# A block's decay tables loaded behind a clear, and two pairs of PSUM banks exchanged

## The chip, the cores and the metric

The kernel runs on one core of a Trainium2 chip. The metric is the device time of one execution in microseconds; three timed executions of the kernel before took 422.1, 422.23 and 422.89, so the median is 422.23. Its engines are named as in the profile: PE is TensorE (the matrix products), PEld its weight loads, DVE is VectorE, ACT is ScalarE, POOL is GpSimd and SP is SyncE, which here only issues transfers.

## What is computed

One transformer block on 256 tokens of width 1024, all in fp32. In the reference, cut to what matters here:

```
mod = silu(c) @ w_ada + b_ada                  # six rows of 1024: shifts, scales, gates
h = x * (1 + sc1) + sh1
proj = h @ w_in                                # cut into mq mk mv | rq rk rv | rg | g_a g_r
y_a = moba_attention(rotary(mq), rotary(mk), mv)    # 8 heads of 64; one block of 256 keys: causal softmax
y_r = retention(rotate(rq), rotate(rk), rv)         # 4 heads, 128 for queries and keys, 256 for values
y_r = silu(rg) * head_norm(y_r)
y = (sigmoid(g_a) * (y_a @ w_proj_moba) + sigmoid(g_r) * (y_r @ w_proj_ret)) @ w_out
x = layer_norm(alpha * x + g1 * y)
# then a gated feed-forward layer of width 2816 with a short convolution, and a second layer_norm
```

The retention's scores q k^T are multiplied, element by element, by a decay that depends on the distance of the two tokens and on the head, and is zero for later keys. The kernel gets these factors as a table: for each pair of heads 128 partitions with 2 x 384 numbers, 384 KB a pair.

## The kernel before

**Precision and weights.** Every matrix product of the big layers is made of three products of rounded parts: a weight tile comes from HBM as fp32 into a buffer named raw (five of them, 1 MB each), ScalarE copies it rounded into whi, VectorE subtracts and writes the rest into wlo. Activations are split in the same way (AH holds the high and low part of the modulated x; AYa and AYb, A2a and others hold further pairs).

**The start** (L161 to L416). SP issues the weights in a fixed order; the first modulation weights go out by ScalarE's queue. `load_A` fills the five raw buffers and issues x's transposed tiles (AYa<-in_xT, L197) between them. A few products on data that nobody reads (L228, L249) keep TensorE busy till the first weights are there. VectorE computes the modulation of x's first tile with four multiply-and-sum instructions (L274) and a sum (L278), scales x with it (L303), and the products of `x_prod` (L337) begin. They need the high part of the weights (L320), their low part (L323), and the low part of x (L308, L310).

Where the first weights' tile is loaded by ScalarE's queue, the kernel writes one column of it with VectorE first (L210). The load writes the same tile, so it is ordered behind that write.

**The main list.** Behind the start, `main` is a list of 1 MB weight loads and `steps` a list of functions with the products for each half of a load. A loop (L1335) goes through the steps; in each it calls the generators in `sides` three times, prepares the halves that come due some steps later (L1279, L1293), and calls the step's function. All engines get their instructions in the order in which this loop makes them; semaphores hold an instruction back until what it reads has been written and what it overwrites has been read. The first 16 steps are the rotated queries and keys (L134, L138), the next the gates and output projections (L123 to L125).

**The generators.** `mixers` waits for step 7 (SCORES_AT), then issues the decay loads from GpSimd's queue (L1037), and goes on with the attention: scores (L1050), masked maxima (L1059), softmax, transposes, and in the end `attend` (L1072), whose two results lie in PSUM banks 5 and 6 and are split into high and low part by ScalarE (L100) and VectorE (L101). The decays' place in SBUF has no earlier user, and GpSimd has nothing else to do in the meantime.

`retention` follows. Its scores (L1169) of heads 0 and 1 are put into banks 4 and 7, those of heads 2 and 3 into banks 0 and 1. VectorE multiplies them by the decays (L1172), ScalarE and VectorE split them (L1173, L1177), and the value products of head g, nine to a head (`mm3`, so L123 to L125), go into bank VALUES[g], from which ScalarE reads them (L1153). A bank can be written anew when its last reader is through. Behind the value products GpSimd loads x again (L1181).

Of the kernel before, what the change touches and what calls it, by code (L numbers as in the profile page):

```python
# [68 lines left out]
def _body(nc, a, out, pe, act, dve, sp, cst, wts, big, tmp, ps, dram):  # L69
    f = lambda ap: ap.bitcast(F32)  # L70

    def bank(i):
        return ps.tile([128, 512], F32, tag=f"P{i}", name=f"P{i}")
# [6 lines left out]
    def reopen(dt, *names):  # L80
        for n in names:
            pairs[n] = big.tile([128, 2, 2048 if n == "H" else 1024], dt, tag=f"A{n}", name=f"A{n}")

    def slot(n, shape, dt=F32):
        if n in pairs:
            assert pairs[n].dtype == dt
            return pairs[n].rearrange("p e (k t) -> p e k t", k=shape[2])
        if n not in place:
            return big.tile(shape, dt, tag=f"A{n}", name=f"A{n}")
        pair, e = place[n]  # L90
        assert pairs[pair].dtype == dt
        v = pairs[pair][:, e, :math.prod(shape[1:])]
        return v.rearrange("p (a b) -> p a b", a=shape[1]) if len(shape) == 3 else v
# [5 lines left out]
    def split(hi, lo, src):  # L99
        act.activation(hi, src, AF.Copy)  # L100
        dve.tensor_tensor(lo, src, f(hi), OP.subtract)  # L101
# [210 lines left out]
    whl, S = {}, {}  # L312
# [716 lines left out]
    def mixers():  # L1029


        for _ in range(3 * SCORES_AT):
            yield
        v = S["v"]
        S["decay"] = [slot(n, [128, 2, 384]) for n in ("D0", "D1")]
        for i in range(2):
            nc.gpsimd.dma_start(S["decay"][i], a["decay"][i])  # L1037
        st, pt = {}, {}
        blk = [slice(128 * qb, 128 + 256 * qb) for qb in range(2)]

        def scores(h):


            S["sc"] = [bank(b) for b in (4, 7, 5, 6)]
            x = S["rot"][h // 4]
            for qb, c in enumerate(blk):
                for i in range(2):
                    for e in range(4):
                        s = slice(32 * e, 32 * e + 32)
                        pe.matmul(S["sc"][e][:, c], x[s, i, qb * 128:(qb + 1) * 128], x[s, 2 + i, :128 + 128 * qb],  # L1050
                                  start=i == 0, stop=i == 1)

        def maxima(h):

            for e in range(2):
                sm = S["sms"][:, (h + e) % (TL + 2)]
                mx = tmp.tile([128, 8], F32, name="mx", bufs=TL + 2)
                for qb, c in enumerate(blk):
                    dve.tensor_tensor_reduce(out=sm[:, c], in0=S["sc"][h % 4 + e][:, c],  # L1059
                                             in1=consts["mask"][:, 128 - 128 * qb:],  # L1060
                                             scale=-0.125, scalar=3.0e38, op0=OP.add, op1=OP.min,
                                             accum_out=mx[:, 2 + qb:3 + qb])
                st[h + e] = sm, mx

        def attend(h, p):

            for w in range(2):
                pT = [pt.pop(h + 2 * w + e) for e in range(2)]
                for kb, (o, c) in enumerate(((slice(0, 256), slice(0, 256)), (slice(128, 256), slice(256, 384)))):
                    for e in range(2):  # L1070
                        u = h + 2 * w + e
                        pe.matmul(p[64 * e:64 * e + 64, 256 * w + o.start:256 * w + o.stop],  # L1072
                                  v[:, kb, 64 * u:64 * u + 64], pT[e][:, c], start=kb == 0, stop=kb == 1)
            return lambda: split(S["yah"][:, h // 2:h // 2 + 2], S["yal"][:, h // 2:h // 2 + 2],
                                 p.rearrange("p (w t) -> p w t", w=2))

        for i in range(HM + 5):
            yield
            if 0 <= i - 3 < HM:
                sm, mx = st[i - 3]  # L1080
                for qb, c in enumerate(blk):
                    act.activation(sm[:, c], sm[:, c], AF.Copy, scale=mx[:, 6 + qb:7 + qb])
            if i == 7:
                for t in range(2):
                    act.activation(S["rvx"][0][t], S["rv"][t], AF.Copy)
            if 0 <= i - 1 < HM:
                sm, mx = st[i - 1]
                for qb, c in enumerate(blk):
                    act.activation(sm[:, c], sm[:, c], AF.Exp, scale=-1.0, bias=mx[:, 2 + qb:3 + qb],
                                   accum_out=mx[:, 4 + qb:5 + qb])  # L1090
            yield
            if 0 <= i - 1 < HM:
                dve.reciprocal(mx[:, 6:8], mx[:, 4:6])
            if i == HM + 4:
                S["yah"], S["yal"] = [slot(n, [128, 4, 256], F32R) for n in ("5", "15")]
                done = [attend(4 * g, bank(5 + g)) for g in range(2)]
            for h in {6: (0, 1), 9: (2, 3, 4, 5), 11: (6, 7)}.get(i, ()):
                sm, mx = st.pop(h)
                p = bank((4, 7, 4, 7, 5, 6, 4, 7)[h])
                for b in range(3):  # L1100
                    pe.transpose(p[:, b * 128:(b + 1) * 128], sm[:, b * 128:(b + 1) * 128], ident)
                pT = sm if h > 1 else slot(("9a", "9b")[h], [128, 384])
                act.activation(pT, p[:, :384], AF.Copy)
                pt[h] = pT
            if i == 0:
                S["sms"] = slot(11, [128, TL + 2, 384])
            if i in (0, 4):
                scores(i)
            if i == 4:
                reopen(F32R, "Ya", "Yb")  # L1110
                S["rvx"] = [[pairs["Y" + e][:, t] for t in range(2)] for e in "ab"]
            if i in (0, 2, 4, 6):
                maxima(i)
            if i == RET_AT:
                sides.append(retention())
            yield
        for fn in done:
            fn()

    def retention():  # L1120
        rot, decay, sms = S["rot"][2:], S["decay"], S["sms"]
# [2 lines left out]
            yield  # L1124
            yield
        rv, (rvh, rvl) = S["rv"], S["rvx"]
        SCORES, VALUES = ((4, 7), (0, 1)), (5, 6, 4, 7)
        mv = tmp.tile([128, 3, 8], F32, name="mvr", bufs=1)
        square = decay[0][:, 0, :256]
        sd = tmp.tile([128, 8], F32, name="sdr", bufs=1)  # L1130
# [189 lines left out]
    prep_to(FIRST + 2)  # L1320
    evac_B()
    sides = [mixers()]

    def run_sides():
# [148 lines left out]
```

## Time and profile before

| | before |
|---|---|
| median of three runs | 422.23 us |
| the profiled execution's own time | 421.75 us |
| its span | 420.0 us |
| TensorE busy | 412.0 us (98%) |
| VectorE busy | 374.2 us (89%) |
| ScalarE busy | 255.5 us (61%) |
| moved by transfers | 105.73 MB, mean 252 GB/s |
| TensorE's waits for another engine | L228 1.6, L337 1.2, L123 0.8, L885 0.4 us |

The span is that of the program's own instructions; the execution's time is 1.75 us longer. In the rows of the profile stand start and length in us, the engine, the line of the kernel, the operation, and what it writes and reads, with an arrow; x4 is a group of four, whose length is that of the whole group; "[1.61 <-DMA ...]" is the time for which the engine stood before it, and what ended that. The queue q1 is SP's, q10 ScalarE's, q0 GpSimd's. In the list of waits stand the instruction that waited, the one that released it, and the time in total, the number of waits and the longest. The chain that ended last is followed back from the last instruction, at each step to what released it.

### The profile page before, as it was taken

The page shows a single profiled execution, that of the slowest core. Times are in us where ns is not written, and L with a number is a line of the kernel's source. Part 1 is how long each engine was busy: PE and PEld are TensorE (multiplying, and loading weights), DVE is VectorE, ACT ScalarE, POOL GpSimd, SP SyncE. Part 2 cuts the span into 40 slices and gives each one's busy share as a digit, 9 for nine tenths or more (in the row PEclk, how much of TensorE's full clock was granted, in tenths as well). Part 3 has the DMA queues.
Part 4 walks back from the last instruction along what each step waited for, and adds up shares of the span by engine and source line. Part 5 has one row for each costly group of instructions (what it writes and reads, how often), then busy time and mean ns, then how long its engine had stood idle before and what let it go on. Part 6 is the DMA issues. An engine that isn't in the chain of part 4 may idle for free.

```text
span 420.0 us, 5974 instructions
## 1 busy us (share of the span) xinstructions
PE 412.0 (98%) x2168; PEld 346.7 (83%) x2168; DVE 374.2 (89%) x599; ACT 255.5 (61%) x448; POOL 14.0 (3%) x26
## 2 busy tenths in 40 slices
PE   7999999999999999999999999999999999999995
PEld 3888888888887888888888898888888888888884
DVE  4897997789999879999887889899999998789996
ACT  3767577769896896626554886363564555455700
POOL 1000000000000100001000000100000000003200
PEclk9999999999999999999999999999999999999999
DMA  8999999744754788999772073895867877420002
GB/s 299 406 411 412 415 415 411 278 176 145 282 209 192 305 292 312 378 343 370 260 292 101 2 300 115 316 364 213 307 249 245 307 295 257 188 101 2 1 3 99
DMA packets 18685, 105.73 MB, mean 252 GB/s; under 512 B 2272, under 2 KB 3680, under 8 KB 7904
## 3 DMA queue, kind: packets, MB, share of 16 engines
q1 hardware_dynamic: 17136, 99.84, 62.8%
q0 software_dynamic: 1376, 4.99, 3.3%
q10 hardware_dynamic: 144, 0.52, 0.5%
q8 instruction: 17, 0.28, 0.3%
q14 instruction: 12, 0.10, 0.1%
HBM read 104.28 MB, written 1.06 MB: 251 GB/s over the span
## 4 chain that ended last, share of the span: by engine, by line
PE 85%; DVE 11%; DMA 2%; issue 1%; SPq 0%; DVEq 0%; ACT 0%; ACTq 0%
PE P L134 21%; PE P L337 13%; PE P L123 12%; PE P L124 12%; PE P L125 12%; PE P L138 11%; DVE wlo L1293 3%; DMA AYa<-in_xT 2%; DVE junk L263 2%; DVE A L1059 1%; PE P L721 1%; PE P L723 1%; PE P L724 1%; DVE A8a L1008 1%; DVE AR L1010 1%
## 5 line engine op out<-in xcount | busy, mean ns | idle before, releaser
L1293 DVE TENSOR_TENSOR wlo<-raw,whi 128x1024 fp32r<-128x1024 f32 x118 | 141.7, 1219 | 14.9 <-ACT whi L1279 14.8
L1279 ACT ACTIVATE whi<-raw 128x1024 fp32r<-128x1024 f32 x118 | 121.0, 1055 | 26.4 <-PE P L125 14.8
L134 PE MATMUL P<-AYa,whi 128*128 128x512 f32 x160 | 46.3, 391 | 0.0
L337 PE MATMUL P<-whi,AH 128*128 128x512 f32 x160 | 41.9, 391 | 1.2 <-DVE AH L303 1.2
L134 PE MATMUL P<-AYb,whi 128*128 128x512 f32 x160 | 43.0, 390 | 0.0
L263 DVE CUSTOM_DVE_ANT_0 junk<-raw,srow 128x1024 bf16<-128x1024 f32 x32 | 38.9, 1217 | 0.0
L123 PE MATMUL P<-whi,AH 128*128 128x512 f32 x96 | 37.9, 394 | 0.0
L125 PE MATMUL P<-whi,AH 128*128 128x512 f32 x96 | 37.4, 390 | 0.0
L124 PE MATMUL P<-wlo,AH 128*128 128x512 f32 x96 | 37.4, 389 | 0.0
L337 PEld LDWEIGHTS P<-whi,AH 128*128 128x128 f32 x160 | 29.8, 188 | 8.8 <-ACT whi L320 2.4
L134 PEld LDWEIGHTS P<-AYb,whi 128*128 128x128 f32 x160 | 30.0, 188 | 6.7
L134 PEld LDWEIGHTS P<-AYa,whi 128*128 128x128 f32 x160 | 28.8, 189 | 4.7
L481 ACT ACTIVATE A<-P 128x256 f32<-128x256 f32 x40 | 15.1, 377 | 28.9 <-PE P L138 19.6
L134 PE MATMUL P<-AH,whi 128*128 128x512 f32 x128 | 31.6, 394 | 0.0
L320 ACT ACTIVATE whi<-raw 128x512 fp32r<-128x512 f32 (+1 forms) x26 | 20.8, 824 | 17.4 <-DMA raw<-in_b 16.0
L323 DVE TENSOR_TENSOR wlo<-raw,whi 128x512 fp32r<-128x512 f32 (+1 forms) x26 | 23.6, 936 | 5.1 <-ACT whi L320 4.6
L134 PEld LDWEIGHTS P<-AH,whi 128*128 128x128 f32 x128 | 23.3, 188 | 5.1 <-issue 0.3
L138 PE MATMUL P<-AYb,wlo 128*128 128x256 f32 x160 | 25.7, 283 | 0.0
L138 PE MATMUL P<-AYa,wlo 128*128 128x256 f32 x160 | 25.6, 283 | 0.0
L138 PEld LDWEIGHTS P<-AYa,wlo 128*128 128x128 f32 x160 | 23.3, 190 | 1.6
L337 PE MATMUL P<-wlo,AH 128*128 128x512 f32 x80 | 23.2, 390 | 0.0
L810 DVE SCALAR_TENSOR_TENSOR A<-A,tables 128x255 f32<-128x255 f32 (+1 forms) x44 | 21.3, 484 | 1.6
(325 smaller groups left out, 774.7 us busy)
## 6 DMA issues: line engine op xcount, KB each, us to landing
raw<-in_ada SPq DMA_DIRECT2D x16, 1024.0 KB, 5.5
raw<-in_wup SPq DMA_DIRECT2D x11, 1024.0 KB, 6.8
raw<-in_wgate SPq DMA_DIRECT2D x11, 1024.0 KB, 6.8
raw<-in_wdown SPq DMA_DIRECT2D x11, 1024.0 KB, 4.9
raw<-in_wrot SPq DMA_DIRECT2D x8, 1024.0 KB, 8.3
raw<-in_m SPq DMA_DIRECT2D x4, 1024.0 KB, 9.8
raw<-in_b SPq DMA_DIRECT2D x4, 1024.0 KB, 9.6
raw<-in_winGr SPq DMA_DIRECT2D x4, 1024.0 KB, 5.4
```

What stands on the lines that cost most here:

```text
L123: pe.matmul(o, lh, rh, start=start, stop=False)
L124: pe.matmul(o, lh, rl, start=False, stop=False)
L125: pe.matmul(o, ll, rh, start=False, stop=stop)
L134: pe.matmul(banks()[half], t[0][:, k * 128:(k + 1) * 128], x2(k), start=k == 0, stop=half > 0 and k == 7)
L138: pe.matmul(banks()[half][:, :256], t[1][:, k * 128:(k + 1) * 128], x2(k)[:, 0], start=False, stop=half == 0 and k == 7)
L263: dve.tensor_tensor_reduce(out=nobody(j if own else None), in0=raw, in1=srow, scale=1.0, scalar=0.0, op0=OP.mult, op1=OP.add, accum_out=mo ...
L320: act.activation(hi[:, o], raw[:, o], AF.Copy)
L323: dve.tensor_tensor(lo[:, o], raw[:, o], f(hi[:, o]), OP.subtract)
L337: pe.matmul(pa[b0 + c // 512 * 2 + t], x[xi][:, j, t * 128:(t + 1) * 128], ws[k][:, c:c + 512], start=first and (xi, k) == (0, 0), stop=la ...
L810: dve.scalar_tensor_tensor(g[:, 2 - n:], x[:, :254 + n], w(n), g[:, 2 - n:], op0=OP.mult, op1=OP.add)
L1279: act.activation(hi, src, AF.Copy)
L1293: dve.tensor_tensor(lo, src, f(hi), OP.subtract)
```

## The change

Two lines. Each half of the decays' tile is written in one column by VectorE before GpSimd's load, so that the load is ordered behind VectorE's instruction at that place of the program (the start of step 7). And the value products of the retention's heads 0 and 1 go to banks 4 and 7, those of heads 2 and 3 to banks 5 and 6, where it was the other way round.

```
@@ mixers
         S["decay"] = [slot(n, [128, 2, 384]) for n in ("D0", "D1")]
         for i in range(2):
+            dve.memset(S["decay"][i][:, 0, :1], 0.0)
             nc.gpsimd.dma_start(S["decay"][i], a["decay"][i])
@@ retention
         rv, (rvh, rvl) = S["rv"], S["rvx"]
-        SCORES, VALUES = ((4, 7), (0, 1)), (5, 6, 4, 7)
+        SCORES, VALUES = ((4, 7), (0, 1)), (4, 7, 5, 6)
```

Nothing that is computed changes.

More of the change, by code (lines that the diff above doesn't have):

```diff
@@ L1036, in mixers @@
         for i in range(2):
+            dve.memset(S["decay"][i][:, 0, :1], 0.0)
             nc.gpsimd.dma_start(S["decay"][i], a["decay"][i])
@@ L1126, in retention @@
         rv, (rvh, rvl) = S["rv"], S["rvx"]
-        SCORES, VALUES = ((4, 7), (0, 1)), (5, 6, 4, 7)
+        SCORES, VALUES = ((4, 7), (0, 1)), (4, 7, 5, 6)
         mv = tmp.tile([128, 3, 8], F32, name="mvr", bufs=1)
```

## The prediction

> **What bounds the kernel now.** I read the page first, for the engine that is never free.
>
> ```profile
> PE 412.0 (98%) x2168; PEld 346.7 (83%) x2168; DVE 374.2 (89%) x599; ACT 255.5 (61%) x448; POOL 14.0 (3%) x26
> ...
> PEclk9999999999999999999999999999999999999999
> ...
> GB/s 299 406 411 412 415 415 411 278 176 145 282 209 192 305 292 312 378 343 370 260 292 101 2 300 115 316 364 213 307 249 245 307 295 257 188 101 2 1 3 99
> ```
>
> TensorE works for 412.0 of 420.0 us, so only two things can shorten the kernel: less work on TensorE, which this change doesn't bring, or less of the 8 us in which it stands. The last line says that the transfers run at over 400 GB/s in slices 1 to 6 (10.5 to 73.5 us) and have room after that. So I asked next for whom TensorE waits, and then for the chain that ended last.
>
> ```profile
> PE P L337 <- DVE AH L303: 1.2, 1, 1.2
> PE P L123 <- DVE A L101: 0.8, 1, 0.8
> ```
>
> ```profile
> 2.17 7.03 DMA AYa<-in_xT
> 9.29 0.36 DVE AH L303
> 9.78 55.11 PE P L337 x240
> ...
> 89.00 0.34 DVE A L1059
> ...
> 135.08 0.70 DVE A L101
> 135.91 0.35 PE P L123
> ```
>
> There are two waits that the change can touch. The chain opens with the transfer of the first x tile, which lands at 9.20, 7.03 us after its issue; VectorE scales it and TensorE starts at 9.78, with products 55.11 / 240 = 0.23 apart. From 89.00 to 135.78 the chain runs through VectorE, which is then without a pause, and at 135.91 TensorE waits for VectorE's split of the attention's result (L101). After 135.91 the chain stays on TensorE to its last products. A microsecond gained at either place is therefore a microsecond of the end, if nothing else comes due in it.
>
> **Part 1: the decays leave the start.** Before, GpSimd issues both decay loads with nothing to wait for, at the very beginning, although only the retention's scores (L1172) read them.
>
> ```profile
> 1.44 1.26 POOL L1037 DMA_DIRECT2D AD<-in_decay  x2
> ...
> 5.15 3.42 PE L249 MATMUL P<-raw 128*128 128x512 f32 x4
> ...
> 7.51 0.16 DVE L278 TENSOR_REDUCE mod<-sums 128x2 f32<-128x6 f32 x1
> ...
> 9.29 0.60 DVE L303 TENSOR_SCALAR AH<-AYa,mod 128x128 fp32r<-128x128 f32 x2 [1.61 <-DMA AYa<-in_xT]
> ...
> 9.75 0.63 ACT L320 ACTIVATE whi<-raw 128x512 fp32r<-128x512 f32 x1 [0.98 <-DMA raw<-in_b]
> 9.78 1.39 PE L337 MATMUL P<-whi,AH 128*128 128x512 f32 x4 [1.21 <-DVE AH L303]
> ...
> 10.29 0.58 ACT L242 ACTIVATE srow<-P 128x512 f32<-128x512 f32 x1
> ...
> 10.77 0.59 ACT L308 ACTIVATE A7a<-AYa,mod 128x256 f32<-128x256 f32 x1
> ...
> 11.39 0.42 DVE L310 TENSOR_TENSOR AH<-A7a,AH 128x256 fp32r<-128x256 f32 x1 [0.28 <-ACT A7a L308]
> ...
> 11.93 1.59 PE L337 MATMUL P<-whi,AH 128*128 128x512 f32 x6
> ...
> 134.68 0.39 PE L125 MATMUL P<-whi,AH 128*128 128x512 f32 x1
> ```
>
> The DMA view of 5.4 to 8.6 us tells what the decays take, and the two us behind it what SP's queue moves alone:
>
> ```profile
> DMA packets 510, 1.29 MB, mean 405 GB/s; under 512 B 74, under 2 KB 202, under 8 KB 510
> ...
> q0 software_dynamic: 160, 0.79, 60.3%
> q1 hardware_dynamic: 350, 0.51, 43.1%
> ```
>
> ```profile
> q1 hardware_dynamic: 402, 0.79, 106.9%
> ```
>
> All 0.79 MB of the decays (queue q0) are moved in those 3.2 us, ahead of most of SP's queue (q1). Without them q1 has 0.79 MB / 405 GB/s = 1.95 us more, and it can use them, since alone it moves 0.79 MB in 2.0 us, 395 GB/s. Everything that lands on q1 after 8.6 comes 1.95 us earlier. What starts TensorE then, in order:
>
> - x lands at 9.20 - 1.95 = 7.25. The modulation that L303 also needs is ready at 7.51 + 0.16 = 7.67; I leave it there, since the next item holds TensorE in any case. L303 starts at about 7.7, and the first product could follow 0.49 later (9.78 - 9.29), at 8.2.
> - TensorE is then still in the warm-up products of L249, which end at 5.15 + 3.42 = 8.57. A following product starts about 0.16 before its forerunner's end (the row at 134.68 is 0.39 long, and one starts each 0.23). First product: 8.41, so 1.37 earlier.
> - The third product needs the other half of the weights: L320 at 9.75 - 1.95 = 7.80, done at 8.43, needed at 8.41 + 2 x 0.23 = 8.87. No wait; now it is one.
> - The ninth product needs x's low part (L310). Now it starts at 11.93, which is 2.15 after the first, where eight products need 8 x 0.23 = 1.84. Scalar's row L320, L242, L308 without a pause, then L310 (ends at 11.81), all hang on the landing at 9.75 and move by 1.95: ready at 9.86. TensorE comes at 8.41 + 1.84 = 10.25. So the ninth product moves from 11.93 to 10.25: **1.68 us**.
>
> Behind that, TensorE is 1.68 earlier and its supply 1.95, so no later wait gets tighter. I take 1.68; bounds 1.37 (the first product's gain, nothing regained behind it) and 1.95 (the whole transfer time).
>
> Where the decays go: the clears are issued at the start of step 7, behind step 6's splits, so in VectorE's pause before it reads the first scores:
>
> ```profile
> 0.90 0.06 DVE L210 MEMSET raw<- 128x1 f32 x1
> ...
> 85.03 2.35 DVE L1293 TENSOR_TENSOR wlo<-raw,whi 128x1024 fp32r<-128x1024 f32 x2
> ...
> 88.70 0.29 DVE L1059 CUSTOM_DVE_ANT_0 A<-P,tables 128x128 f32<-128x128 f32 x1 [1.31 <-PE P L1050]
> ...
> 131.34 1.95 DVE L1172 TENSOR_TENSOR A<-P,AD 128x384 f32<-128x384 f32 x4
> ```
>
> Two clears cost 2 x 0.06 = 0.12 us of a pause of 1.31: nothing; without that cover 0.12. GpSimd waits from 1.4 to about 86 on a clear; behind it in its queue stands only the load of x behind the value products (L1181). VectorE is through with step 6's splits at 85.03 + 2.35 = 87.38; with the 1.26 of the issue and 7.03, as x took under full load, the decays land by 87.4 - 1.7 + 1.26 + 7.03 = 94, and L1172 reads them at 131.34 - 1.7 = 129.6, so 35 us are spare. Their 1.95 us of transfer now fall beside the loads of that time. The last that they can touch:
>
> ```profile
> 91.06 0.33 SPq L110 DMA_DIRECT2D raw<-in_winB  x1
> ...
> 101.16 2.01 ACT L1279 ACTIVATE whi<-raw 128x1024 fp32r<-128x1024 f32 x2
> ```
>
> Issued at 91.06, it lands by 98.1 even if it takes x's 7.03, and Scalar splits it at 101.16: 3 us spare against 1.95. Nothing.
>
> [...]
>
> **Part 2: the banks.** No instruction is added; two pairs of value products swap banks.
>
> ```profile
> 133.21 1.02 DVE L1177 TENSOR_TENSOR A<-A,A2a 128x384 fp32r<-128x384 f32 x2
> ...
> 135.08 1.28 DVE L101 TENSOR_TENSOR A<-P,A 128x512 fp32r<-128x512 f32 x2
> 135.91 0.35 PE L123 MATMUL P<-AYa,A2a 128*128 128x256 f32 x1 [0.84 <-DVE A L101]
> ...
> 141.88 0.69 DVE L528 TENSOR_TENSOR A<-P,A 128x512 f32<-128x512 f32 x1 [0.76 <-PE P L125]
> ```
>
> Products stand 0.23 apart before the gap, so head 0's first could start at 134.91; it starts at 135.91, since bank 5 still holds attention that L101 reads until 135.78. In bank 4 it waits for the scores' reader L1172, done at 133.29, and for the decayed scores of L1177, done for heads 0 and 1 at 134.23. Both are past: **1.00 us** gained. What is late next: a head's nine products are half as wide (256), by estimate 0.115 each and 1.04 together, so head 2 comes to bank 5 at 134.91 + 2 x 1.04 = 136.99, and L101 is through with it at 135.78; head 3 comes to bank 6 at 138.03, free at 135.08 + 1.28 = 136.36. The spare is 1.21 us, so the bank wait isn't moved on but gone. VectorE is not behind for long: at 141.88 it waits 0.76 for TensorE. Bounds: 0.84 (the idle time) and 1.00.
>
> **The sum.** 1.68 + 1.00 = 2.68 us. The profiled execution took 421.75 for a span of 420.0; it becomes 419.07 for 417.3. The median of the runs, 422.23, stands 0.48 above that execution; the same gain makes it 419.55, forecast **419.5**. What a measurement here can tell from no change is 0.2%, 0.84 us.
>
> **Rivals.**
>
> *A, the start's gain isn't there* (421.2, only part 2). x was late because SP's own queue is long: it lands 7.03 after its issue, behind all that SP asked for first. Then the time of q0 would go to later requests, with no earlier x. [...] Against: the two DMA views. 7 in 100.
>
> *B, another wait in the place of L101's* (420.5, only part 1). The weight load before head 0 could be held by something the view doesn't name, say the last L1177, done just ahead of L101 at 135.08. Against: head 0 doesn't read that. 6 in 100.
>
> *C, the earlier products run at half rate* (420.2). TensorE starts slower than it goes on:
>
> ```profile
> L240 PE MATMUL P<-ident,sc x8: 421/421/421, 3.4 to 4.9; 128*128 128x128 f32 x8
> ...
> L1214 PE MATMUL P<-ident,A8a x8: 272/272/273, 170.2 to 171.4; 128*128 128x128 f32 x8
> ...
> L249 PE MATMUL P<-raw x4: 593/1040/1061, 5.1 to 8.0; 128*128 128x512 f32 x4
> ```
>
> The same transposes take 421 ns at 3.4 us and 272 later, though the clock row of the page shows full speed. If the first products still ran slow at 8.41, they would lose at most half of the 1.37 us up to 9.78, where products stand at the full pace: 0.68, so 419.5 + 0.68 = 420.2. Against: the last warm-up product, at 8.0, takes 593 where the others take 1040, so the full rate is there before 8.41, and nothing up to then is moved. 4 in 100. [...]
>
> *D, slower: VectorE falls behind at step 7* (423 and more). The clear, then GpSimd's descriptors and 0.79 MB beside VectorE's dense stretch from 89 to 136. Each us that VectorE is late beyond the new spare of 1.21 at bank 5 is paid by TensorE; slower than before only from 1.21 + 2.68 = 3.9 us, against clears of 0.12 and a GpSimd issue of 1.26. At 5 us it gives 422.2 + 1.1 = 423.3. 2 in 100.
>
> *E, the clear doesn't hold the loads back* (421.2). Against: L210 in the rows above clears a tile ahead of its load in the same way. 1 in 100.
>
> **How the numbers follow.** The forecast has 80 in 100. The range: from 418.8 (1.95 + 1.00, and 0.5 for the runs' own spread) to 420.8 (B or C with 0.3 of spread); A, E and D lie outside, with the forecast's far tails. A and E lie at the edge of what can be told (1.0 against 0.84), so about half of them counts as the same: faster 0.91, same 0.06, slower 0.03.
>
> **What would show it.** Decay loads issued near 86 with a wait for VectorE's clear; no q0 packets before 80; x landing at 7.3, first product at 8.4, ninth at 10.2; no wait of L123 on L101; head 0's first product 0.23 behind its forerunner; the same order of loads behind. It is wrong if x still lands past 8.5, if TensorE stops anew before 75 us, or if the value products wait for another reader.

## The result, and the profile after

The median after is 418.9 us (six runs, 418.65 to 419.11); before 422.54 us in the runs beside it (six, 422.07 to 423.21). The ratio is 0.9913, its 95% interval 0.99 to 0.9926. The forecast was 419.5 in a range of 418.8 to 420.8. The profiled execution took 419.11 for a span of 417.4, where 419.07 and 417.3 were forecast.

The page of the kernel after, the lines that answer to those of before:

```profile
PE 410.7 (98%) x2168; PEld 346.5 (83%) x2168; DVE 373.9 (90%) x601; ACT 255.5 (61%) x448; POOL 14.0 (3%) x26
...
PEclk9999999999999999999999999999999999999998
...
GB/s 291 406 411 414 416 414 407 232 272 163 249 232 171 347 264 360 373 353 340 280 252 100 8 296 145 309 373 211 298 269 224 321 289 257 185 95 2 1 5 97
```

VectorE has two instructions more, the clears; the bytes are the same. Slice 8 (84 to 94 us, counted from 0), with 176 GB/s before, now has 272: there the decays are. For whom TensorE waits, after:

```profile
PE P L228 <- DVE srow L226: 1.6, 1, 1.6
PE P L337 <- DVE AH L303: 0.7, 1, 0.7
PE P L885 <- ACT AYb L883: 0.4, 1, 0.4
```

The wait of L123 on L101 is gone, and the wait at L337 is 0.7 instead of 1.2. The chain that ended last has changed with it: it is TensorE's for 96% of the span (85% before), and VectorE's stretch from 89 to 136 no longer stands in it. The start, in the timeline after:

```profile
5.16 2.42 PE L249 MATMUL P<-raw 128*128 128x512 f32 x4
...
7.64 0.16 DVE L278 TENSOR_REDUCE mod<-sums 128x2 f32<-128x6 f32 x1
7.83 0.60 DVE L303 TENSOR_SCALAR AH<-AYa,mod 128x128 fp32r<-128x128 f32 x2
7.88 0.63 ACT L320 ACTIVATE whi<-raw 128x512 fp32r<-128x512 f32 x1 [0.36 <-DMA raw<-in_b]
...
8.32 1.17 PE L337 MATMUL P<-whi,AH 128*128 128x512 f32 x4 [0.74 <-DVE AH L303]
...
10.26 1.54 PE L337 MATMUL P<-whi,AH 128*128 128x512 f32 x6
```

L303 waits no longer for x (no bracket), but follows the modulation (L278) at once. x landed 5.0 us after its issue at 2.18, instead of 7.03 after 2.17. The DMA view of 5.4 to 8.6 us after has q1 alone:

```profile
DMA packets 711, 1.19 MB, mean 373 GB/s; under 512 B 81, under 2 KB 209, under 8 KB 711
...
q1 hardware_dynamic: 711, 1.19, 105.2%
```

Where the decays went, and head 0's value products:

```profile
83.48 2.35 DVE L1294 TENSOR_TENSOR wlo<-raw,whi 128x1024 fp32r<-128x1024 f32 x2
85.79 0.07 DVE L1037 MEMSET AD<- 128x1 f32 x2
87.15 0.29 DVE L1060 CUSTOM_DVE_ANT_0 A<-P,tables 128x128 f32<-128x128 f32 x1 [1.30 <-PE P L1051]
...
86.16 1.26 POOL L1038 DMA_DIRECT2D AD<-in_decay  x2 [84.78 <-DVE AD L1037]
...
133.14 0.39 PE L125 MATMUL P<-whi,AH 128*128 128x512 f32 x1
133.37 0.28 PE L123 MATMUL P<-AYa,A2a 128*128 128x256 f32 x1
```

The two clears lie in VectorE's pause, GpSimd waited 84.78 us for them, and head 0's first product follows its forerunner at 0.23 us.

Laid side by side, product by product, TensorE of after is ahead of before by 1.46 us at the first product (9.78 and 8.32), 1.67 at the ninth (11.93 and 10.26), 1.5 from 17 us on, and by 2.54 from head 0's first value product (135.91 and 133.37) on. At the end of the span it is 2.6.

So the profiles give 2.6 us, and the medians 3.6. The other 1 us is not in these two profiles; the experiments had to find it.

### The profile page after: what moved, and what is told of

Its sections match the earlier page's. It is cut to its first block, busy times and chain, and to the rows that moved or that the text cites. A ratio compares the mean times of both kernels' runs of the same rounds, so it can differ in the third digit from the quotient of the medians.

```text
span 417.4 us, 5973 instructions
## 1 busy us (share of the span) xinstructions
PE 410.7 (98%) x2168; PEld 346.5 (83%) x2168; DVE 373.9 (90%) x601; ACT 255.5 (61%) x448; POOL 14.0 (3%) x26
## 3 DMA queue, kind: packets, MB, share of 16 engines
q0 software_dynamic: 1376, 4.99, 3.1%
## 4 chain that ended last, share of the span: by engine, by line
PE 96%; DVE 1%; DMA 1%; issue 0%; DVEq 0%; ACT 0%; ACTq 0%
PE P L134 25%; PE P L337 13%; PE P L123 13%; PE P L125 13%; PE P L124 13%; PE P L138 13%; DMA raw<-in_m 1%; PE P L721 1%; PE P L723 1%; PE P L724 1%; PE P L1051 1%; PE P L1170 1%; PE P L1073 1%; PE P L1102 1%; DVE unread L274 1%; PE P L665 0%
## 5 line engine op out<-in xcount | busy, mean ns | idle before, releaser
L337 PE MATMUL P<-whi,AH 128*128 128x512 f32 x160 | 41.9, 391 | 0.7 <-DVE AH L303 0.7
L123 PE MATMUL P<-whi,AH 128*128 128x512 f32 x96 | 37.9, 394 | 0.0
L337 PEld LDWEIGHTS P<-whi,AH 128*128 128x128 f32 x160 | 29.8, 188 | 8.2 <-ACT whi L320 1.5
L320 ACT ACTIVATE whi<-raw 128x512 fp32r<-128x512 f32 (+1 forms) x26 | 20.8, 824 | 15.5 <-DMA raw<-in_b 14.1
L337 PE MATMUL P<-wlo,AH 128*128 128x512 f32 x80 | 23.2, 390 | 0.0
```

The costliest lines, as they stand in the source:

```text
L123: pe.matmul(o, lh, rh, start=start, stop=False)
L320: act.activation(hi[:, o], raw[:, o], AF.Copy)
L337: pe.matmul(pa[b0 + c // 512 * 2 + t], x[xi][:, j, t * 128:(t + 1) * 128], ws[k][:, c:c + 512], start=first and (xi, k) == (0, 0), stop=la ...
```

## The experiments

My theory: the decays' bytes stood ahead of x and the first weights, and bank 5's reader L101 held head 0. Its rival came up with the profile after. The granted clock is the share of its full clock that TensorE gets; in these traces it is 1.00 or 0.50. Its record begins with the rise to 1.00, at 7.81 us in the profile before and at 5.59 in that after, and the four warm-up products of L249 agree with it: they take 3.42 us before and 2.42 after. So the start might owe its gain to an earlier clock.

**The parts, one by one.** `clears_alone` is after without the exchange of banks, `banks_alone` after without the clears:

```
clears_alone:  SCORES, VALUES = ((4, 7), (0, 1)), (5, 6, 4, 7)
banks_alone:   -            dve.memset(S["decay"][i][:, 0, :1], 0.0)
```

> The clears without the exchange of banks. If the two parts add up as in the prediction: first product near 8.4 us, ninth near 10.25, head 0's first value product again held by L101 for about 1.0 us; span 1.6 us below that of before. If part 2 had no share in the gain, the span is 2.6 us below.

> The exchange of banks without the clears. By the prediction: x lands near 9.2 and the first product starts near 9.8, as before; no wait of L123 on L101; span 1.0 us below that of before. By the rival that the earlier clock (granted at 5.59 us after, at 7.81 before) made the gain at the start: if the clock is granted early here too, the first product starts near 8.4 and the span is 2.6 us below.

`clears_alone` took 420.04 (six runs, 419.9 to 420.18), a ratio of 0.9945 (0.993 to 0.996). Its span is 418.2, so 1.8 below that of before where 1.6 was expected; its first product stands at 8.36, its ninth at 10.30, and the list of its waits has L123 on L101 again:

```profile
PE P L337 <- DVE AH L303: 0.9, 1, 0.9
PE P L123 <- DVE A L101: 0.8, 1, 0.8
```

`banks_alone` took 420.94 (twelve runs, 420.78 to 421.98), a ratio of 0.9969 (0.9957 to 0.9981). There is no wait on L101, the first product starts at 9.83, and so x lands at about 9.25 (0.58 ahead of it, as in the profile before, 9.20 and 9.78): as predicted. But its span in the profile is 420.3 and not 419.0, and the reason is in the windows of its profile. A row has the stretch and its length in us, then the busy time and the number of instructions of PE, PEld, DVE, ACT and POOL, then the granted clock, the share of the DMA engines and GB/s:

```profile
6.64:10.05 3.41, 1.63 (x4) 0.54 (x4) 1.92 (x8) 0.83 (x3) 0.00 (x0) 1.00 1.03 392
10.05:13.47 3.42, 3.42 (x9) 2.48 (x9) 2.90 (x5) 3.42 (x6) 0.00 (x0) 0.50 1.04 411
13.47:16.88 3.41, 3.41 (x17) 2.77 (x16) 3.22 (x4) 2.32 (x6) 0.00 (x0) 1.00 1.03 404
```

From 10.05 to 13.47 the clock is halved: TensorE does 9 products in 3.42 us where it does 17 in the next stretch. Its ninth product comes at 13.33, 1.40 later than in the profile before. So the rival is half right: the clock matters at the start, but not as it said.

**The kernel before, once more.**

> The kernel before, once more, since its times spread from 422.07 to 423.21 where those after the change spread from 418.65 to 419.11. If the spread comes from the mixing of the decays' packets with SP's, the landing of x moves by up to 1 us from 9.20 and the rest with it. If it comes from the clock, x lands at 9.2 and products run slow past 9.8.

It took 421.86, its span is 420.2. The clock is granted at 5.41, as early as after, and still the first product starts at 9.75, so that x lands at about 9.17 by the same 0.58. That refutes the rival: an early clock brought nothing while x wasn't there. The spread that I asked about did not show in this one run.

The times of before beside the three sets of experiments, 43 runs, show it: 27 of them, with a mean granted clock of 0.997 and more, took 421.54 to 422.26 (median 421.86); 16, with 0.994 to 0.996, took 422.83 to 423.41 (median 423.1). `banks_alone` falls apart likewise: nine runs from 420.78 to 421.21 and three from 421.80 to 421.98 with 0.995. None of twelve runs of after does, nor any of the six of `clears_alone`. No profile of the kernel before itself fell into its second group; what such a run looks like is taken from `banks_alone`, whose start is the same.

**The pause ahead of the first product.** If a pause of TensorE halves the clock, filling it in the kernel before must remove the second group, and lengthening it in the kernel after must bring it in. Only the number of warm-up products (L247) is changed:

```
before_filled:  BUSY = 3        # before has 2
after_thinned:  BUSY = 1        # after has 2
after_bare:     BUSY = 0
```

> The kernel before with one more pair of warm-up products (BUSY = 3). Before's 17 runs of the last comparison fall into two groups: 10 of 421.54 to 422.25 with a mean clock of 0.997 and more, 7 of 422.83 to 423.41 with 0.994 to 0.996. If the second group comes from the pause ahead of the first product (2.3 us in one profile, and in another run with a pause of 1.7 the clock was halved from 10.05 to 13.47 us), a shorter pause removes it: all runs between 421.4 and 422.4, median near 421.8. If the groups have another cause, both are there again, the median stays near 422.2.

> The kernel after with one pair of warm-up products fewer (BUSY = 1), so that its pause ahead of the first product grows from 0.7 us to 1.4 or more, with nothing else moved. If the pause halves the clock for a window of 3.4 us, some runs are 1.0 to 1.5 us slower, with a mean clock near 0.995, and others stay near 418.9. If not, all runs stay between 418.6 and 419.2.

> After with no warm-up products that wait for weights (BUSY = 0): TensorE stands from about 5.4 to 8.3. If a pause in a 3.4 us window halves the clock, or keeps it from being granted, nearly every run now has products at half pace up to 12 us or so: 1 to 2 us above after, mean clock 0.995 or less. If the pause as such costs nothing, 418.9 as after.

`before_filled`: 421.9, eleven runs from 421.61 to 422.32, all with a clock of 0.997 and more; of before's fifteen runs beside them three took 422.98 to 423.35. `after_thinned`: four runs from 418.8 to 419.1, and one of 420.23 with 0.995; its pause is 1.1 us in the profile (one of the four), not the 1.4 expected. `after_bare`: 420.3 (420.14 to 420.38), all four runs with 0.995 or 0.996. Its windows:

```profile
5.03:8.45 3.42, 0.40 (x3) 0.19 (x2) 3.35 (x12) 1.71 (x4) 0.00 (x0) 1.00 1.03 389
8.45:11.86 3.41, 3.41 (x9) 2.74 (x9) 3.06 (x6) 3.09 (x6) 0.00 (x0) 0.50 1.03 416
11.86:15.27 3.41, 3.41 (x17) 2.78 (x16) 3.38 (x6) 2.62 (x5) 0.00 (x0) 1.00 1.03 404
```

All three fit. In the two profiles that show it, a stretch of 3.41 us that begins where the clock is granted (6.64 in `banks_alone`, 5.03 in `after_bare`), with TensorE busy for 1.63 and 0.40 us of it, is followed by one of 3.42 and 3.41 us at a granted clock of 0.50. `after_bare` carries it, four runs of four against none of twelve of after. For `after_thinned` it is one run in five, a weak leg, and eleven runs of `before_filled` without a loss are weak against three of fifteen beside them, though clearer against 16 of 43.

The other kernels add to it, sorted by the pause ahead of the first product in a profile of each: up to 1.0 us none of 42 runs has a clock under 0.997, at 1.1 us one of 11 (`after_thinned`, `m0_quarters`), at 1.2 to 2.3 us 19 of 56 (`before`, `before_again`, `banks_alone`), at 3.0 us all four. The pause's length alone doesn't decide a run: `before_again` kept the clock with 2.26 us (7.49 to 9.75), which lay across the end of the stretch at 8.82, and `banks_alone` lost it with 1.72 us (8.11 to 9.83) that lay in one.

Where the limit is, two profiles that kept the clock and two that lost it narrow down. First stretches of `before_again`, and of after:

```profile
5.41:8.82 3.41, 2.02 (x4) 0.36 (x3) 2.23 (x9) 1.06 (x2) 0.00 (x0) 1.00 1.04 404
```

```profile
5.59:9.00 3.41, 2.61 (x7) 0.95 (x6) 3.34 (x13) 2.24 (x5) 0.00 (x0) 1.00 1.06 381
9.00:12.42 3.42, 3.42 (x17) 2.70 (x16) 2.66 (x6) 3.02 (x6) 0.00 (x0) 1.00 1.01 407
```

Busy for 2.02 of 3.41 us (59%) kept the clock, for 1.63 (48%, `banks_alone`) lost it. Where the stretches begin differs from run to run: at 4.77 us in the earliest of these profiles (`m0_quarters`), at 7.81 in the latest. By my estimate from these shares some of before's stretches, with a pause between 1.2 and 2.3 us, then fall under the limit, though no profile of before shows one that did. After, the pause is 0.7 us in one profile and 0.1 in the other (`after_again`, from 8.14 to 8.22), and the first stretches are busy for 2.61 and 3.29 us.

**How much the bytes count.** One decay early, the other behind its clear:

```
             for i in range(2):
+                if i:
                     dve.memset(S["decay"][i][:, 0, :1], 0.0)
```

> After, with a clear ahead of the second decay load alone: 0.39 of the 0.79 MB go out at the start again. If the bytes ahead of x set the start, x lands near 8.2 (half of 1.95 later), the first product starts near 8.75, the ninth near 11.0; the median is 0.6 to 0.9 us above that of after. If any load of GpSimd at the start is the trouble, all of the 1.7 us comes back; if the amount doesn't matter, none.

419.8 (four runs, 419.66 to 420.12), 0.8 to 0.9 above after. L303 waits for x again:

```profile
8.12 0.60 DVE L303 TENSOR_SCALAR AH<-AYa,mod 128x128 fp32r<-128x128 f32 x2 [0.47 <-DMA AYa<-in_xT]
```

x lands at about 8.03 (0.09 ahead of L303, as before: 9.20 and 9.29), the first product stands at 8.61, the ninth at 10.90, where 8.2, 8.75 and 11.0 were expected. x comes 0.85 us later for 0.39 MB than after (7.18), and 2.02 for 0.79 MB (9.20): the cost grows with the bytes.

**When the loads may come.** `decays_in_flood` has the clears and loads in the start's loop, in the middle of the dense stretch of transfers; `by_sp` has no clears, and SP's queue issues the loads at the place of the program that they have after:

```
decays_in_flood (behind raws.pop("a2") at L394, and not in mixers):
+    S["decay"] = [slot(n, [128, 2, 384]) for n in ("D0", "D1")]
+    for i in range(2):
+        dve.memset(S["decay"][i][:, 0, :1], 0.0)
+        nc.gpsimd.dma_start(S["decay"][i], a["decay"][i])
by_sp:
-            dve.memset(S["decay"][i][:, 0, :1], 0.0)
-            nc.gpsimd.dma_start(S["decay"][i], a["decay"][i])
+            sp.dma_start(S["decay"][i], a["decay"][i])
```

> After, with the clears and the loads near 30 us, in the stretch from 10 to 73 us where transfers run at over 400 GB/s, instead of near 86. If only the start is short of bytes, TensorE has its weights far enough ahead: no new wait, same median as after (418.9). If each byte in that stretch is on the path, a wait for whi or wlo of up to 1.95 us shows between 30 and 75 us.

> After, with no clears: the decay loads are issued by SP's queue at the same place of the program. If it is only the time of the loads that counts, the same as after within 0.3 us. If the clear or GpSimd's queue matters by itself, or two more issues in SP's order hold up the weights, it is slower by 0.5 us or more.

`decays_in_flood`: 418.86 (four runs, 418.83 to 419.25), the same as after. The loads went out at 36.09:

```profile
36.09 1.26 POOL L398 DMA_DIRECT2D AD<-in_decay  x2 [34.72 <-DVE AD L397]
```

No wait for weights came up. `by_sp` issued them at 84.92 and took 419.21 (four runs, 419.01 to 419.28), 0.2 above after's second set of runs beside it, too little to tell from no change. So the clear is a means; what counts is that the loads don't stand ahead of x. Places between the start and 36 us were not tried.

**The spare at the banks.** After with `VALUES = (4, 6, 5, 7)`: head 1 goes to bank 6, whose reader is the second L101.

> After, with head 1 in bank 6 instead of 7 (head 3 goes to 7). Head 1's first product stands at 134.45 in the profile after, and L101 is through with bank 6 at 134.81. If the readers of a bank alone decide, head 1 waits 0.35 to 0.45 us and the span grows by that. If the banks' numbers matter in another way, nothing or 1 us.

```profile
133.34 1.28 DVE L101 TENSOR_TENSOR A<-P,A 128x512 fp32r<-128x512 f32 x2
```

```profile
134.13 0.28 PE L125 MATMUL P<-AYa,A 128*128 128x256 f32 x1
134.67 0.39 PE L123 MATMUL P<-AYa,A2a 128*128 128x256 f32 x1 [0.26 <-DVE A L101]
134.90 0.28 PE L124 MATMUL P<-AYb,A2a 128*128 128x256 f32 x1
```

Head 1's first product stands 0.54 behind its forerunner instead of 0.12, so 0.42 are lost, about what the reader's end (134.62) against the place in line (134.25) makes expect, 0.37. The only run took 419.46, with a span of 417.7. By this profile the bank's reader decides, and not its number.

**After once more, and an attempt to go on.** L303 now follows the modulation, whose first sum (L274, at 4.99) waits for the first 512 KB of weights. `m0_quarters` cuts these in two:

```
-PIECES = dict(m0=(0, 1024, 2048), b0=(0, 512, 1024, 1536, 2048))
+PIECES = dict(m0=(0, 512, 1024, 2048), b0=(0, 512, 1024, 1536, 2048))
```

> The kernel after once more, as the measure for the other three: 418.6 to 419.2, no run with a mean clock under 0.997, and 2.9 to 3.2 us below the faster group of before's runs.

> After, with the first half of the first modulation weights loaded as two pieces of 256 KB (the second by SP's queue) instead of one of 512 KB. In the profile after, VectorE's first sum starts at 4.99, held by the landing of that piece, while the transposed rows that it also needs are done at about 4.5; the first product follows from it. If that landing sets the start now, the sums begin 0.3 to 0.5 us earlier and the kernel gains as much: 418.4 to 418.6. If SP's queue, one issue longer, gives it back (x 0.4 later, at 7.6), nothing: 418.9.

`after_again`: 418.99 (six runs, 418.85 to 419.16), all with 0.997 and more; 2.9 below before's group of the full clock (421.86). `m0_quarters`: 419.77 (419.23 to 420.37), so slower by 0.8. Its first sum starts at 4.55, but the third waits for the second half of the weights:

```profile
6.22 0.69 DVE L274 CUSTOM_DVE_ANT_0 unread<-P,raw 128x512 bf16<-128x512 f32 x1 [0.36 <-DMA raw<-in_m]
...
8.23 0.63 ACT L320 ACTIVATE whi<-raw 128x512 fp32r<-128x512 f32 x1 [0.77 <-DMA raw<-in_b]
8.26 1.16 PE L337 MATMUL P<-whi,AH 128*128 128x512 f32 x3 [1.08 <-DVE AH L303]
```

The sums end no earlier, L303 starts at 7.77 instead of 7.83, and what SP issues behind comes later: the weights of the third product at 8.23 instead of 7.88. At the ninth product this is 0.16 us (10.42 against 10.26) of the 0.4 by which the span is longer; the rest, and why three of its six runs took 420.04 and more at a full clock, stays open. No version here beats after.

## Why the prediction was right, point by point

- *The decays' bytes stand ahead of x.* Right in kind and size: x lands at 7.18 (forecast 7.25), and `one_decay_early` shows it by halves. How little SP's queue got beside GpSimd's goes with the packets, the pieces in which the profile counts a transfer (queue, packets, MB, share of the DMA engines). From 6 to 7 us in the profile before the two queues moved about equally many, but GpSimd's carried 5.6 KB each and SP's 1.3:

```profile
q0 software_dynamic: 66, 0.37, 88.3%
q1 hardware_dynamic: 62, 0.08, 20.8%
```

- *What starts TensorE then.* The time was right, 8.32 (8.41), for the wrong reason. I had the warm-up products hold TensorE until 8.57. They end at 7.58 after, since the clock rose 2.2 us earlier in that run; the holder was the modulation, which I had put at 7.67 and which came at 7.80. By my own sum its path led to 8.2; that the two holders lie so close together, and the error stays under 0.1 us, is luck. In `decays_in_flood` the warm-ups end at 8.38 (5.16 and 3.22), which by the 0.16 of my sum leads to 8.22, and the first product starts at 8.27.
- *The ninth product at 10.25.* It came at 10.26: a gain of 1.67 (1.68).
- *Behind that, the supply is 1.95 earlier, so no later wait gets tighter.* This was a little wrong. In the timelines below, first before and then after, ScalarE's split ahead of the second x tile (L320) starts at 15.14 where before it starts at 16.60, 1.46 earlier and not 1.95; the weight load at 16.74 has to wait 0.38 for it and for L305 behind it, and the lead falls from 1.67 to 1.5. Part of it is that q1 alone moved 1.19 MB in the 3.2 us in which 1.29 were moved before: 0.10 MB are 0.25 us at the 405 GB/s of before's view. The rest isn't settled. The lead also differs between executions: `clears_alone`, where L101 still holds head 0's first product, ends 1.8 ahead of before (418.2 against 420.0).

```profile
16.60 1.06 ACT L320 ACTIVATE whi<-raw 128x1024 fp32r<-128x1024 f32 x1 [1.20 <-DMA raw<-in_b]
```

```profile
15.14 1.06 ACT L320 ACTIVATE whi<-raw 128x1024 fp32r<-128x1024 f32 x1 [1.21 <-DMA raw<-in_b]
16.11 0.59 ACT L305 ACTIVATE AH<-AYb,mod 128x256 fp32r<-128x256 f32 x1
...
16.74 0.76 PEld L337 LDWEIGHTS P<-whi,AH 128*128 128x128 f32 x4 [0.38 <-ACT AH L305]
```

- *The clears cost nothing, the decays come in time.* Right: 0.07 us in a pause of 1.30, and the second load landed at about 92 against a use at 129.79. That the place is free is shown by `decays_in_flood` as well.
- *The banks bring 1.00.* Right: 1.00 in the profile, 0.98 between the medians of `banks_alone` and before at the full clock (420.88 and 421.86), 1.1 between `clears_alone` and after. The spare at bank 5 came out at 1.31 (head 2 at 135.52, L101 through at 134.21), where I had 1.21; that a bank's reader is what a spare is counted from, `bank_spare` shows.
- *The sum.* 2.68 forecast; 2.64 between the profiled executions (421.75 and 419.11), 2.96 between the medians at the full clock (421.86 and 418.9). The 0.3 between these lies within the groups' spread: before's profiled execution is 0.11 below its group's median, after's 0.21 above. The medians of all runs differ by 3.6. The term that was missing is the share of before's runs that are slower by 1.27 us (423.1 - 421.86), at a mean granted clock of 0.994 to 0.996. By their times, two of my three runs belong to the first group (422.1 and 422.23) and one to the second (422.89), and the six beside the result are three and three, so that their median, 422.54, lies between the groups, where no run is. The 0.48 that I put on top of the profiled execution had no counterpart after; it is most of the 0.6 by which 419.5 is above 418.9.
- *The rivals.* A, B, D and E did not come. C had the half rate, on the wrong side: I asked whether TensorE at half rate could spoil the gain, and bounded it by 0.68; but the runs with a mean clock under 0.997 came with the longer pause, 16 of 43 of the kernel before, and of twelve runs of after there was none.

## What to carry to other kernels

A load that waits for nothing can go out at once, wherever the program has it: here at 1.44 us, though it stands at step 7. Where the start was short of bytes it cost about its own transfer time: x came 2.02 us later for 0.79 MB, which are 1.95 us at 405 GB/s. A wait that put it behind the first demand gave that back, at 36 us as well as at 86. A bank is free by its last reader's place in that reader's queue: bank 5 was held until 135.78, bank 4's reader was through at 133.29, and the exchange brought 1.00 us. So give the next product the bank whose reader comes first. And where a kernel's times fall into groups, look at the granted clock before taking a median for the truth: in `banks_alone` a pause of TensorE of 1.72 us at the start was followed by 3.42 us at a clock of 0.50, and the three of its runs with a mean clock of 0.995 took 1.05 us longer than the others (medians 421.93 and 420.88).

## What was not expected of the hardware

At the start, TensorE's granted clock was 0.50 for a stretch of 3.41 us after one in which TensorE was busy for 48% (`banks_alone`) and for 12% (`after_bare`), and it stayed at 1.00 after one of 59% (`before_again`) and more (77% after, 96% in `after_again`). Of the 43 runs of the kernel before, the 16 with a mean clock of 0.994 to 0.996 took 1.27 us longer than the others; of the twelve runs of after, with a pause of 0.7 us or less in the profiles instead of 1.2 to 2.3, none had a mean clock that low. To get the full clock may take more than to keep it: in the profile before TensorE was busy for 2.81 of the 3.41 us from 0.98 to 4.39 (82%), and the full clock stands in the record only from 7.81 on; in `m0_quarters` it was busy for 3.19 of the 3.41 us from 1.36 to 4.77 (94%), and had it from 4.77 on. That is an estimate from these two profiles: it takes it that stretches of 3.41 us lie ahead of the record's begin as well, which no run shows.
